# Cross-attention's queries called a unit ahead, and value differences made from rows copied one row down by DMA

## The chip, the cores and the metric

The kernel runs on one core of one Trainium2 chip. The metric is device time in microseconds (us) of one execution, and the time before is the median of three runs.

The core has five engines with their own instruction queues: PE (matrix multiplications and transposes), DVE (vector), ACT (scalar), POOL and SP. In this kernel SP only issues DMA transfers, mostly loads; POOL computes a little and issues nearly all stores. Each engine takes its instructions strictly in the order of its queue: an instruction that waits holds all behind it. The transfers themselves are moved by 16 DMA engines that SP's and POOL's queues share.

## What is computed

One layer of a hybrid encoder, for a prompt of 2048 rows and a sample of 64 rows, all in float32:

```python
h = rms_norm(x, g_norm)
z = h @ w_in                      # 24 chunks of 128 columns: q, k, v, gate of branch A; u, gate of B; q, gate of C
o_sb   = stick_breaking(q_sb, k, v)             # branch A, 8 heads of 64
o_pool = multiscale_pool(u) @ pool_w * scale    # branch B
o_xa   = softmax(q_xa @ mk.T / 8) @ mv          # branch C: cross-attention to 256 memory rows, 4 heads of 64
y = rms_norm(x + concat[o_sb*silu(g_sb), o_pool*silu(g_pool), o_xa*silu(g_xa)] @ w_out, g_final)
```

The new keys and values (rows by head) are outputs too. In branch A the kernel does not use the values themselves but the differences between neighbouring rows, `v[t-1] - v[t]` (with a row of zeros ahead of the first), so that the running products of the stick-breaking weights need no further multiplication.

## The kernel before, in words

**Split products.** Float32 products are made of three passes of PE with the operands split into a high and a low part (lines 427 to 429). One "piece" is such a product for one of the 8 slices of the contraction; a "block" is 8 pieces (24 multiplications): one chunk of 128 columns of z for 512 rows of the prompt. Four blocks (n = 0 to 3) make a chunk; the last is wider, as the sample's 64 rows go with it.

**The stage that is changed** makes 4 chunks of keys and then 4 chunks of values: 32 blocks, 16 of keys and 16 of values. After a block of keys or values, ACT copies the accumulator to SBUF (`zf`, `zv`), POOL stores it transposed as it is (`vt_d`), PE turns it into rows (`pt_r`, line 463), ACT copies these rows to the tile `rt` (line 465), and POOL stores them to the output. The tile `rt` has **one buffer**, so ACT's next copy to it waits until all readers of the last one are done. The accumulator and most others have two.

**Value differences before.** POOL subtracts neighbouring columns of the transposed values (`dz`, line 564; the first column comes from the block before by a small copy on DVE, line 556), PE turns the result into rows with four more transposes (`pt_d`, line 570), ACT copies them (line 571), and POOL stores them to `dv_d` (line 572).

**Cross-attention** is interleaved with these blocks in 16 units of 256 query rows and two heads: scores (line 764, 765), softmax (DVE, ACT), transposes (`pt_p`), products with the memory values (`avx`), a gate on POOL and a store. The queries were stored earlier to `qx_d` and are loaded by SP (line 748). Each load of 256 KB reads 64 rows twice, through a leading dimension of size 2 and step 0, so that both halves of the 128 partitions get the same queries. Two such loads (one for each head) and one of the gate (`sg_x`, line 751) make a unit's loads.

**What sets the order.** A small helper, `Slots`, counts pieces: `slots.after(d, f)` runs `f` d pieces later. A unit starts with every second block (16 pieces), its stages follow after the delays in XSLOTS, and the next unit's loads are called 12 pieces after a unit's start. Behind this, the framework's scheduler orders each engine's queue, moves instructions by its own estimates, and adds the semaphore waits. After the values a new set of buffers is opened for the sample's work, which waits for the stage's last users.

Of the kernel before, what the change touches and what calls it, by code (L numbers as in the profile page):

```python
# [8 lines left out]
F32 = mybir.dt.float32  # L9
F32R = mybir.dt.float32r  # L10
# [3 lines left out]
ALU = mybir.AluOpType  # L14
# [4 lines left out]
P = 128  # L19
# [9 lines left out]
NB = T // 512  # L29
UNIT = 256  # L30
# [7 lines left out]
def f(ap):  # L38

    return ap.bitcast(F32)  # L40
# [3 lines left out]
def tile_hybrid_step(  # L44
# [30 lines left out]
    V, A, G, PE = nc.vector, nc.scalar, nc.gpsimd, nc.tensor  # L75
    dma, store = nc.sync.dma_start, nc.gpsimd.dma_start
# [7 lines left out]
    v_new = sb_v_prompt[0, 0].rearrange("t h d -> t (h d)")  # L84
# [11 lines left out]
    ident = edge[:, 384:]  # L96
# [9 lines left out]
    vt_d = [dram.tile([P, T], F32, name=f"vt_d{p}") for p in range(4)]  # L106
    sg_d = [dram.tile([P, T], F32, name=f"sg_d{p}") for p in range(6)]
# [56 lines left out]
    def join(av, out, odd):  # L164

        own, other = (HI, LO) if odd else (LO, HI)
        A.copy(out[own], av[other])
        V.tensor_tensor(out[own], av[own], out[own], ALU.add)
# [81 lines left out]
    class Stream:  # L250
# [35 lines left out]
        def piece(self):  # L286

            if not self.pieces:
                self.pieces += self.more()
            if self.pieces:  # L290
                thunk = self.pieces.pop(0)
                if thunk is not None:
                    thunk()
                    return True
            return False
# [40 lines left out]

    slots, ROWS, XSLOTS = Slots(), 2, (1, 7, 13, 16, 17, 20)


    hpool = ctx.enter_context(tc.tile_pool(name="hpool", bufs=1))
# [2 lines left out]
    ps_t = ctx.enter_context(tc.tile_pool(name="ps_t", bufs=2, space=PSUM))  # L345
# [17 lines left out]
    st = st0 = scope.enter_context(tc.tile_pool(name="st0", bufs=2))  # L363
# [34 lines left out]
    def load_ahead():  # L398

        if order:  # L400
            c = order.pop(0)
            loaded[c] = split_weights(win[:, c * P : (c + 1) * P].rearrange("(k p) m -> p k m", p=P), wpool)

    def chunk_of(c):
        while c not in loaded:
            load_ahead()
        return loaded.pop(c)
# [42 lines left out]
    def project(w, n, chunk):  # L450
        for piece in projection(w, n, chunk):
            acc = piece()
            slots.tick()
        return acc

    def halves(t):
        return t.rearrange("p (a b) -> p a b", a=2)

    def rows_of(src, out, n_tiles):

        pt = ps_t.tile([P, 4, P], F32, tag="pt", name="pt_r")
        for j in range(n_tiles):
            PE.transpose(pt[:, j], src[:, j * P : (j + 1) * P], ident)
        rt = st.tile([P, n_tiles, P], F32, tag="rt", name="rt", bufs=1)
        A.copy(rt[:, :n_tiles], pt[:, :n_tiles])
        store(out.rearrange("(j p) c -> p j c", p=P), rt[:, :n_tiles])
        return rt
# [56 lines left out]
    def tokens(n):  # L524
        return slice(512 * n, 512 * n + 512)
# [24 lines left out]
        slots.after(ROWS, lambda: rows_of(zf, k_new[tokens(n), p * P : (p + 1) * P], 4))  # L550

    def values(acc, n, p):

        zv = st.tile([P, 1 + 512], F32, tag="zf", name="zv")
        if n:
            V.tensor_copy(zv[:, 0:1], last_values[0][:, 512:])
        else:
            V.memset(zv[:, 0:1], 0.0)
        last_values[:] = [zv]
        A.copy(halves(zv[:, 1:]), acc)  # L560
        store(vt_d[p][:, tokens(n)], zv[:, 1:])
        two = st.tile([P, 2, 512], F32, tag="s", name="dv")
        dz, dr = two[:, 0], two[:, 1].rearrange("p (j c) -> p j c", j=4)
        G.tensor_tensor(dz, zv[:, :512], zv[:, 1:], ALU.subtract)

        def rows():
            rows_of(zv[:, 1:], v_new[tokens(n), p * P : (p + 1) * P], 4)
            pt = ps_t.tile([P, 4, P], F32, tag="pt", name="pt_d")
            for j in range(4):
                PE.transpose(pt[:, j], dz[:, j * P : (j + 1) * P], ident)  # L570
            A.copy(dr, pt)
            store(dv_d[p][:, n], dr)

        slots.after(ROWS, rows)

    last_values = []

    mxs = normed([mem_prompt[0, :P, :]], P, gm, "m0", lambda: dma(gm, g_mem[0:1, :].broadcast_to([P, D])))
    mxs += normed([mem_prompt[0, P:, :]], P, gm, "m1")
# [16 lines left out]
    for n in range(NB):  # L596
        turns = norm_group(n + 1) if n + 1 < NB else []
        for p in range(2):
            pieces = projection(w2[p], n, QX0 + p)
            for k, piece in enumerate(pieces):  # L600
                acc = piece()
# [10 lines left out]
    st = scope.enter_context(tc.tile_pool(name="st1", bufs=2))  # L612
# [22 lines left out]
    for c in range(2):  # L635
        for j in range(2):
            w, rows = WINDOWS[2 * c + j], slice(64 * j, 64 * j + 64)
# [65 lines left out]
    for c in range(2):  # L703
        w = chunk_of(U0 + c)
        last, pls = None, []
        for n in range(NB):
            acc = project(w, n, U0 + c)
            u = st.tile([P, HIST + 512], F32, tag="u", name="u")
# [12 lines left out]
        for n in (3, 0, 1, 2):  # L721
            acc = project(w, n, GP0 + c)
            sg = st.tile([P, 512], F32, tag="zf", name="sg_p")
# [14 lines left out]
    st = scope.enter_context(tc.tile_pool(name="st2", bufs=2))  # L738
    xa = mscope.enter_context(tc.tile_pool(name="xa", bufs=1))

    def cross_loads(p, u):

        cols = slice(UNIT * u, UNIT * u + UNIT)
        qx = []
        for j in range(2):
            q = xa.tile([P, 2, UNIT], F32R, tag=f"q{j}", name="qx", bufs=2)
            src = qx_d[p][HI if j else LO, :, cols]
            dma(f(q), src.unsqueeze(0).broadcast_to([2] + list(src.shape)))
            qx.append(q)
        sg = xa.tile([P, UNIT], F32, tag="sg", name="sg_x", bufs=2)  # L750
        dma(sg, sg_d[4 + p][:, cols])
        return qx, sg

    def cross(p, u, loads):

        qx, sg = loads
        pr, turned = [None] * 2, [None] * 2
        o = xa.tile([P, UNIT], F32, tag="ox", name="ox")

        def scores(i):  # L760
            q = slice(P * i, P * i + P)
            s = ps_x.tile([P, 2, NMEM], F32, tag="x", name="sx")
            for j in range(2):
                PE.matmul(s[:, j], qx[j][:, 0, q], mks[2 * p + j], start=True, stop=False)
                PE.matmul(s[:, j], qx[j][:, 1, q], mks[2 * p + j], start=False, stop=True)
            pr[i] = xa.tile([P, 2, NMEM], F32, tag=f"pr{i}", name="pr")
            softmax(s, P, pr[i])

        def turn(j):
            pt = ps_t.tile([P, 2, 2, P], F32, tag="pt", name="pt_p")  # L770
            for b in range(2):
                for i in range(2):
                    PE.transpose(pt[:, b, i], pr[i][:, j, b * P : (b + 1) * P], ident)
            ph = xa.tile([P, 2, UNIT], F32R, tag="ph", name="ph")
            pl = xa.tile([P, 2, UNIT], F32R, tag="plo", name="plo")
            ptf = pt.rearrange("p b i q -> p b (i q)")
            A.copy(ph, ptf)
            V.tensor_tensor(pl, ptf, f(ph), ALU.subtract)
            turned[j] = ph, pl

        def gather(j):
            av = ps_x.tile([P, 512], F32, tag="y", name="avx")
            ph, pl = turned[j]
            for b in range(2):
                mv = mvs[p][:, b, 2 * j : 2 * j + 2].rearrange("p a d -> p (a d)")
                PE.matmul(av[:, :UNIT], mv, ph[:, b], start=(b == 0), stop=False)
                PE.matmul(av[:, :UNIT], mv, pl[:, b], start=False, stop=(b == 1))
            join(av[:, :UNIT], o, j)
            if j:
                G.tensor_tensor(o, o, sg, ALU.mult)  # L790
                store(mix_d[u // 2][:, 6 + p, UNIT * (u % 2) : UNIT * (u % 2) + UNIT], o)

        for delay, stage, i in zip(XSLOTS, (scores, scores, turn, gather, turn, gather), (0, 1, 0, 0, 1, 1)):
            slots.after(delay, lambda stage=stage, i=i: stage(i))

    crosses = [(p, u) for p in range(2) for u in range(T // UNIT)]
    loads = cross_loads(*crosses[0])

    def next_cross():
        def ahead():  # L800
            nonlocal loads
            if crosses:
                loads = cross_loads(*crosses[0])

        cross(*crosses.pop(0), loads)
        slots.after(12, ahead)

    for make, c0 in ((keys, K0), (values, V0)):
        for p in range(4):
            w = chunk_of(c0 + p)  # L810
            for n in range(NB):
                if n % 2 == 0:
                    next_cross()
                make(project(w, n, c0 + p), n, p)
                if n == 0:
                    load_ahead()
# [5 lines left out]
    st = scope.enter_context(tc.tile_pool(name="st3", bufs=2))  # L822
# [131 lines left out]
    st = ctx.enter_context(tc.tile_pool(name="st4", bufs=2))  # L954
# [6 lines left out]
    for c0, m0, m in ((G0, 0, 4), (GX0, 6, 2)):  # L961
        sg = st.tile([P, 4, TS], F32, tag="sgs", name="sg_s", bufs=1)
# [52 lines left out]
    loads = []  # L1015
# [183 lines left out]
```

## Time and profile before

| what | value |
|---|---|
| median of 3 runs | 1418.0 us (1412.6 to 1421.86) |
| time of the profiled execution | 1418.25 us |
| span of its instructions | 1416.5 us |
| mean granted TensorE clock | 0.971 of full speed |
| stage of keys and values in the span | about 255 to 545 us |

The profile is of one execution. Its page gives each engine's busy time, the chain of work that ended last, and the costliest groups of instructions. Further views of the same trace answer for a stretch of time: the busy time and granted clock in given windows, who waited for whom, the instructions in order of time, the DMA queues with the packets and bytes that they moved, and the chain of waits. "<-" after an idle time names what ended it.

### The profile page before, as it was taken

The page shows a single profiled execution, that of the slowest core. Times are in us where ns is not written, and L with a number is a line of the kernel's source. Part 1 is how long each engine was busy: PE and PEld are TensorE (multiplying, and loading weights), DVE is VectorE, ACT ScalarE, POOL GpSimd, SP SyncE. Part 2 cuts the span into 40 slices and gives each one's busy share as a digit, 9 for nine tenths or more (in the row PEclk, how much of TensorE's full clock was granted, in tenths as well). Part 3 has the DMA queues.
Part 4 walks back from the last instruction along what each step waited for, and adds up shares of the span by engine and source line. Part 5 has one row for each costly group of instructions (what it writes and reads, how often), then busy time and mean ns, then how long its engine had stood idle before and what let it go on. Part 6 is the DMA issues. An engine that isn't in the chain of part 4 may idle for free.

```text
span 1416.5 us, 19689 instructions
## 1 busy us (share of the span) xinstructions
PE 1305.2 (92%) x7418; PEld 986.6 (70%) x7418; DVE 757.9 (54%) x1315; ACT 553.4 (39%) x1141; POOL 322.6 (23%) x425
## 2 busy tenths in 40 slices
PE   5999999699999999999999989999999989999976
PEld 5788877488888888788876656655665656666554
DVE  7853446154444443243234666657676677787523
ACT  5631110143334442221123545455454555655521
POOL 2111336143444442231001232211110011010031
PEclk9999999799999999999999999999999999999988
DMA  7635253244444444433257853334343343331031
GB/s 230 199 114 161 95 185 110 98 155 152 165 156 155 153 140 138 140 107 127 77 193 242 290 178 130 112 108 139 93 129 102 114 144 96 103 107 56 2 116 70
DMA packets 114682, 190.66 MB, mean 135 GB/s; under 512 B 8450, under 2 KB 73052, under 8 KB 114588
## 3 DMA queue, kind: packets, MB, share of 16 engines
q1 hardware_dynamic: 93772, 119.11, 27.5%
q0 software_dynamic: 20816, 70.30, 13.5%
q8 instruction: 58, 0.95, 0.3%
q14 instruction: 36, 0.29, 0.1%
HBM read 119.10 MB, written 70.29 MB: 134 GB/s over the span
## 4 chain that ended last, share of the span: by engine, by line
PE 50%; issue 19%; DMA 12%; DVE 9%; POOL 6%; ACT 2%; SPq 1%; POOLq 0%; DVEq 0%; ACTq 0%
PE acc L1073 7%; PE acc L427 7%; PE acc L428 7%; PE acc L429 7%; PE av L235 6%; DMA qx<-qx_d 6%; PE pt L221 6%; PE z L198 5%; DVE at_hl L210 2%; PE z L1073 2%; DMA m<-mix_d 2%; POOL psum_w L655 2%; DMA mix_d<-ends 1%; PE pt_x L389 1%; DVE wl L420 1%
## 5 line engine op out<-in xcount | busy, mean ns | idle before, releaser
L427 PE MATMUL acc<-hh,wh 128*128 128x512 f32 (+2 forms) x960 | 360.5, 376 | 6.4 <-DVE sg L529 5.6
L428 PE MATMUL acc<-hl,wh 128*128 128x512 f32 (+2 forms) x960 | 344.0, 358 | 0.0
L429 PE MATMUL acc<-hh,wl 128*128 128x512 f32 (+2 forms) x960 | 342.9, 358 | 0.0
L210 DVE TENSOR_TENSOR_SCAN at_hl<-at_hl,at_hl 128x512 f32<-128x512 f32 x148 | 182.2, 1282 | 58.0 <-ACT at_hl L203 57.9
L427 PEld LDWEIGHTS acc<-hh,wh 128*128 128x128 f32 x960 | 183.3, 191 | 33.5 <-DVE sg L529 7.8
L429 PEld LDWEIGHTS acc<-hh,wl 128*128 128x128 f32 x960 | 182.8, 191 | 24.5 <-issue 0.7
L428 PEld LDWEIGHTS acc<-hl,wh 128*128 128x128 f32 x960 | 183.6, 191 | 20.8 <-issue 3.8
L221 PE MATMUL pt<-edge,at_hl 128*128 128x128 f32 x968 | 150.7, 279 | 13.2 <-ACT at_hl L223 9.3
L221 PEld LDWEIGHTS pt<-edge,at_hl 128*128 128x128 f32 x968 | 114.8, 141 | 58.3 <-ACT at_hl L223 17.8
L235 PE MATMUL av<-more_w,at_hh 128*64 128x512 f32 (+2 forms) x480 | 139.0, 538 | 4.6 <-ACT more_w L223 4.6
L203 ACT ACTIVATE at_hl<-z 128x1024 f32<-128x1024 f32 (+3 forms) x143 | 122.4, 890 | 47.5 <-PE z L198 46.7
L223 ACT COPY more_w<-pt 128x512 f32<-128x512 f32 (+2 forms) x240 | 118.4, 517 | 34.5 <-PE pt L221 32.9
L208 DVE TENSOR_TENSOR_SCAN at_hl<-at_hl,edge 128x128 f32<-128x128 f32 (+3 forms) x116 | 86.7, 805 | 53.8 <-ACT at_hl L203 53.7
L1073 PE MATMUL acc<-at_hh,mh 128*128 128x512 f32 x208 | 95.1, 457 | 10.4 <-DVE xo L1076 10.4
L223 ACT COPY at_hl<-pt 128x512 f32<-128x512 f32 x80 | 43.4, 542 | 129.7 <-PE pt L221 129.7
L1059 POOL TENSOR_TENSOR ml<-m,mh 128x256 fp32r<-128x256 f32 x64 | 53.1, 853 | 148.7 <-ACT mh L1058 148.4
L247 POOL TENSOR_TENSOR ends<-ends 128x512 f32<-128x512 f32 x16 | 21.3, 1332 | 283.3 <-DVE ends L246 193.3
L1073 PE MATMUL acc<-at_hl,mh 128*128 128x512 f32 (+1 forms) x208 | 84.6, 411 | 0.0
L198 PE MATMUL z<-at_hh 64*128 64x512 f32 (+2 forms) x576 | 82.3, 398 | 0.2 <-ACT at_hl L203 0.2
L235 PE MATMUL av<-at_hl,at_hh 128*64 128x512 f32 (+1 forms) x160 | 79.9, 581 | 0.6 <-DVE ends L246 0.6
L1073 PE MATMUL acc<-at_hh,ml 128*128 128x512 f32 x192 | 77.3, 402 | 0.0
L235 PEld LDWEIGHTS av<-more_w,at_hh 128*64 128x64 f32 x480 | 39.9, 139 | 45.9 <-issue 22.0
(257 smaller groups left out, 1887.5 us busy)
## 6 DMA issues: line engine op xcount, KB each, us to landing
at_hh<-k_d SPq DMA_DIRECT2D x40, 512.0 KB
wr<-in_w_in_dram SPq DMA_DIRECT2D x24, 512.0 KB
at_hh<-dv_d SPq DMA_DIRECT2D x40, 256.0 KB
xt_x<-in_x_prompt_dram SPq DMA_DIRECT2D x16, 512.0 KB
qx<-qx_d SPq DMA_DIRECT2D x32, 256.0 KB
k_d<-k POOLq DMA_DIRECT2D x16, 512.0 KB, 6.1
out_dram<-rt POOLq DMA_DIRECT2D x32, 256.0 KB, 5.7
q_d<-q POOLq DMA_DIRECT2D x16, 512.0 KB, 3.0
```

The lines of the kernel that those rows point to most:

```text
L198: PE.matmul(z[:, h, :w], a["q"][rows, part, at], K[rows, keys, :w], start=(part == keys == 0), stop=(part == 1),)
L203: A.activation(c[:, :, :n], z[:, :, :n], AF.Sigmoid, scale=-1.0)
L208: V.tensor_tensor_scan(cc, cc, edge[:, 512 - n :][:, ::-1], 0.0, ALU.mult, ALU.max)
L210: V.tensor_tensor_scan(cc, cc, cc, self.later[i][:, h, 0:1], ALU.mult, ALU.bypass)
L221: PE.transpose(pt[:, i], self.cs[i][:, h, kb * P : kb * P + P], ident)
L223: A.copy(w[:, i0:], pt[:, i0:])
L235: PE.matmul(a["av"][rows, i0 * P :], self.V[:, kb, rows], turned[h][:, i0:], start=(self.diag and kb == 0), stop=(j == 0 and kb == 3),)
L427: PE.matmul(out, wh[:, k], hi, start=(k == 0), stop=False)
L428: PE.matmul(out, wh[:, k], lo, start=False, stop=False)
L429: PE.matmul(out, wl[:, k], hi, start=False, stop=(k == KT - 1))
L1059: G.tensor_tensor(ml, m, f(mh), ALU.subtract)
L1073: PE.matmul(o, m, w, start=(c == i == 0), stop=(c == 7 and i == len(passes) - 1))
```

## The change

Two things are changed in the stage of keys and values.

**Cross-attention.** The loaded queries and gates no longer come from pools but from two fixed buffers each, taken in turn. A unit starts every 15 pieces instead of every 16, the first after 8 pieces; when a unit is started the queries of the following one are called at once. The gate is called by the unit itself, 6 pieces after its start. Most stages of a unit stand one piece nearer to its start than before.

**Value differences.** The four transposes, ACT's copy, DVE's copy of the first column and the subtraction of columns are removed. Instead SP copies the rows tile `rt` one row down, from SBUF to SBUF, into a tile `dr`: rows 0 to 126 to rows 1 to 127 (line 566), the last row of tiles 0 to 2 to the first row of tiles 1 to 3 (line 567), and the last row of tile 3 to the first row of the next block's `dr` (line 569, not for the last block of a chunk). POOL then subtracts `rt` from `dr` (line 570) and stores the result. `rt` still has one buffer.

```diff
--- before.py
+++ after.py
@@ -336,7 +336,7 @@
 
 
 
-    slots, ROWS, XSLOTS = Slots(), 2, (1, 7, 13, 16, 17, 20)
+    slots, ROWS, XSLOTS = Slots(), 2, (1, 6, 12, 15, 16, 19)
 
 
     hpool = ctx.enter_context(tc.tile_pool(name="hpool", bufs=1))
@@ -550,30 +550,29 @@
         slots.after(ROWS, lambda: rows_of(zf, k_new[tokens(n), p * P : (p + 1) * P], 4))
 
     def values(acc, n, p):
-
-        zv = st.tile([P, 1 + 512], F32, tag="zf", name="zv")
-        if n:
-            V.tensor_copy(zv[:, 0:1], last_values[0][:, 512:])
-        else:
-            V.memset(zv[:, 0:1], 0.0)
-        last_values[:] = [zv]
-        A.copy(halves(zv[:, 1:]), acc)
-        store(vt_d[p][:, tokens(n)], zv[:, 1:])
-        two = st.tile([P, 2, 512], F32, tag="s", name="dv")
-        dz, dr = two[:, 0], two[:, 1].rearrange("p (j c) -> p j c", j=4)
-        G.tensor_tensor(dz, zv[:, :512], zv[:, 1:], ALU.subtract)
-
-        def rows():
-            rows_of(zv[:, 1:], v_new[tokens(n), p * P : (p + 1) * P], 4)
-            pt = ps_t.tile([P, 4, P], F32, tag="pt", name="pt_d")
-            for j in range(4):
-                PE.transpose(pt[:, j], dz[:, j * P : (j + 1) * P], ident)
-            A.copy(dr, pt)
+        zv = st.tile([P, 512], F32, tag="zf", name="zv")
+        A.copy(halves(zv), acc)
+        store(vt_d[p][:, tokens(n)], zv)
+
+        if n == 0:
+            above[:] = [st.tile([P, 8, P], F32, tag="s", name="dv")[:, :4]]
+            V.memset(above[0][0:1, 0], 0.0)
+        dr = above.pop()
+        if n < NB - 1:
+            above.append(st.tile([P, 8, P], F32, tag="s", name="dv")[:, :4])
+
+        def rows(nxt=list(above)):
+            rt = rows_of(zv, v_new[tokens(n), p * P : (p + 1) * P], 4)
+            dma(dr[1:], rt[: P - 1])
+            dma(dr[0:1, 1:], rt[P - 1 :, :3])
+            for t in nxt:
+                dma(t[0:1, 0], rt[P - 1 :, 3])
+            G.tensor_tensor(dr, dr, rt, ALU.subtract)
             store(dv_d[p][:, n], dr)
 
         slots.after(ROWS, rows)
 
-    last_values = []
+    above = []
 
     mxs = normed([mem_prompt[0, :P, :]], P, gm, "m0", lambda: dma(gm, g_mem[0:1, :].broadcast_to([P, D])))
     mxs += normed([mem_prompt[0, P:, :]], P, gm, "m1")
@@ -743,17 +742,16 @@
         cols = slice(UNIT * u, UNIT * u + UNIT)
         qx = []
         for j in range(2):
-            q = xa.tile([P, 2, UNIT], F32R, tag=f"q{j}", name="qx", bufs=2)
+            q = xroom(f"q{j}")
             src = qx_d[p][HI if j else LO, :, cols]
             dma(f(q), src.unsqueeze(0).broadcast_to([2] + list(src.shape)))
             qx.append(q)
-        sg = xa.tile([P, UNIT], F32, tag="sg", name="sg_x", bufs=2)
-        dma(sg, sg_d[4 + p][:, cols])
-        return qx, sg
-
-    def cross(p, u, loads):
-
-        qx, sg = loads
+        return qx
+
+    def cross(p, u, qx):
+
+        sg = xroom("sg")
+        slots.after(6, lambda: dma(sg, sg_d[4 + p][:, UNIT * u : UNIT * u + UNIT]))
         pr, turned = [None] * 2, [None] * 2
         o = xa.tile([P, UNIT], F32, tag="ox", name="ox")
 
@@ -793,24 +791,30 @@
         for delay, stage, i in zip(XSLOTS, (scores, scores, turn, gather, turn, gather), (0, 1, 0, 0, 1, 1)):
             slots.after(delay, lambda stage=stage, i=i: stage(i))
 
+    xrings = {
+        name: [xa.tile([P, 2, UNIT] if name != "sg" else [P, UNIT], F32R if name != "sg" else F32, name=f"x{name}{i}") for i in range(2)]
+        for name in ("q0", "q1", "sg")
+    }
+
+    def xroom(name):
+        xrings[name].append(xrings[name].pop(0))
+        return xrings[name][-1]
+
     crosses = [(p, u) for p in range(2) for u in range(T // UNIT)]
-    loads = cross_loads(*crosses[0])
+    called = [cross_loads(*crosses[0])]
 
     def next_cross():
-        def ahead():
-            nonlocal loads
-            if crosses:
-                loads = cross_loads(*crosses[0])
-
-        cross(*crosses.pop(0), loads)
-        slots.after(12, ahead)
-
+        cross(*crosses.pop(0), called.pop(0))
+        if crosses:
+            called.append(cross_loads(*crosses[0]))
+
+
+    for i in range(len(crosses)):
+        slots.after(8 + 15 * i, next_cross)
     for make, c0 in ((keys, K0), (values, V0)):
         for p in range(4):
             w = chunk_of(c0 + p)
             for n in range(NB):
-                if n % 2 == 0:
-                    next_cross()
                 make(project(w, n, c0 + p), n, p)
                 if n == 0:
                     load_ahead()
```

How instructions stand in the queues is shown at three places. First the queue of **SP** in the stretch of the values (`qx`, `xq` are queries, `sg_x`, `xsg` gates, `wr` weights). Before:

```order
L748 DMA qx<-qx_d_78 128x2x256 x2
L411 DMA wr<-in_w_in_dram 128x8x128
L751 DMA sg_x<-sg_d_92 128x256
L748 DMA qx<-qx_d_78 128x2x256 x2
L751 DMA sg_x<-sg_d_92 128x256
```

With the change, for a like stretch (`rt` are the rows, `dv` the tile with the shifted rows):

```order
L747 DMA xq_2341<-qx_d_78 128x2x256
L747 DMA xq_2343<-qx_d_78 128x2x256
L754 DMA xsg_2344<-sg_d_92 128x256
L566 DMA dv<-rt 127x512
L567 DMA dv<-rt 1x16x24
L569 DMA dv<-rt 1x16x8
L411 DMA wr<-in_w_in_dram 128x8x128
L566 DMA dv<-rt 127x512
```

16 copies of 127 rows, 16 and 12 copies of parts of one row now stand between the loads of queries, gates and weights. From the first copy of 127 rows to the last there are five pairs of query loads.

Second the queue of **POOL** for the first block of values. Before:

```order
L561 DMA vt_d_83<-zv 128x512
L564 TENSOR_TENSOR dv<-zv 128x512
L466 DMA out_dram<-rt 128x4x128
L572 DMA dv_d_79<-dv 128x512
L561 DMA vt_d_83<-zv 128x512
```

With the change:

```order
L555 DMA vt_d_83<-zv 128x512
L466 DMA out_dram<-rt 128x4x128
L570 TENSOR_TENSOR dv<-dv,rt 128x512
L571 DMA dv_d_79<-dv 128x512
L555 DMA vt_d_83<-zv 128x512
```

The subtraction now reads the rows and the shifted rows, so it stands behind SP's copies; the next block's store of `zv` stands behind it.

Third the queue of **PE** at the first scores of cross-attention. Before:

```order
L463 MATMUL pt_r<-edge,zf 128x128 x4
L427 MATMUL acc<-hh_128,wh 128x512
L428 MATMUL acc<-hl_132,wh 128x512
L764 MATMUL sx<-mks_137,qx 128x256
L765 MATMUL sx<-mks_137,qx 128x256
L429 MATMUL acc<-hh_128,wl 128x512
```

With the change:

```order
L463 MATMUL pt_r<-edge,zf 128x128 x4
L427 MATMUL acc<-hh_128,wh 128x512
L428 MATMUL acc<-hl_132,wh 128x512
L762 MATMUL sx<-mks_137,xq_2340 128x256
L763 MATMUL sx<-mks_137,xq_2340 128x256
L429 MATMUL acc<-hh_128,wl 128x512
```

The first scores stand at the same place as before; those of the second unit stand 12 multiplications of `acc` later than before, after the rows of the second block.

## Rows read from the trace of the kernel before

**Rows 1.** The page's first lines: span, and busy time and share of engines.
```profile
span 1416.5 us, 19689 instructions
PE 1305.2 (92%) x7418; PEld 986.6 (70%) x7418; DVE 757.9 (54%) x1315; ACT 553.4 (39%) x1141; POOL 322.6 (23%) x425
```

**Rows 2.** Busy time in three stretches (start, keys, values), clock, DMA share, GB/s.
```profile
262.00:292.00 30.00, 16.53 (x68) 12.41 (x69) 6.57 (x17) 7.15 (x18) 4.42 (x5) 0.72 0.26 91
292.00:411.00 119.00, 112.41 (x675) 99.30 (x674) 56.48 (x131) 44.84 (x122) 49.96 (x59) 0.99 0.46 158
411.00:541.00 130.00, 122.57 (x758) 106.29 (x756) 54.62 (x128) 54.50 (x140) 53.02 (x75) 1.00 0.44 148
```

**Rows 3.** Waits of PE, keys stretch: us in total, times, longest us.
```profile
PE sx L764 <- DMA qx<-qx_d: 19.7, 6, 8.5
```

**Rows 4.** PE in order of time: start, us, instruction [idle before it].
```profile
271.55 0.55 PE L764 MATMUL sx<-mks,qx 128*128 128x256 f32 x1 [8.50 <-DMA qx<-qx_d]
...
277.03 0.58 PE L764 MATMUL sx<-mks,qx 128*128 128x256 f32 x1 [3.86 <-DMA qx<-qx_d]
```

**Rows 5.** Waits of PE, values stretch.
```profile
PE pt_d L570 <- POOL dv L564: 5.0, 9, 0.6
PE pt_d L570 <- DVE sm_m L153: 2.6, 3, 0.9
```

**Rows 6.** Groups of PE in the values stretch: count | busy, mean ns.
```profile
L570 PE MATMUL pt_d<-edge,dv 128*128 128x128 f32 x60 | 9.7, 283 | 7.4 <-POOL dv L564 4.8 <-DVE sm_m L153 2.6
```

**Rows 7.** Line 465 in the values stretch: ns min/median/max, first and last start.
```profile
L465 ACT COPY rt<-pt_r x16: 585/585/592, 412.2 to 541.4; 128x512 f32<-128x512 f32 x16
```

**Rows 8.** DMA queues, 277 to 281 us: packets, MB, share of 16 engines.
```profile
DMA packets 184, 0.19 MB, mean 47 GB/s; under 512 B 0, under 2 KB 184, under 8 KB 184
...
q1 hardware_dynamic: 184, 0.19, 13.5%
```

**Rows 9.** DMA queues, 398 to 399 us.
```profile
q0 software_dynamic: 93, 0.31, 80.9%
q1 hardware_dynamic: 46, 0.05, 13.4%
```

**Rows 10.** POOL in order of time, one block of values.
```profile
424.46 0.73 POOL L790 TENSOR_TENSOR ox<-ox,sg_x 128x256 f32<-128x256 f32 x1 [0.46 <-DVE ox L168]
...
428.29 1.05 POOL L564 TENSOR_TENSOR dv<-zv 128x512 f32<-128x512 f32 x1
429.75 0.78 POOL L466 DMA_DIRECT2D out_dram<-rt  x1 [0.41 <-ACT rt L465]
```

**Rows 11.** Chain of waits, end of the stage: start, us, what.
```profile
545.73 2.71 DMA mix_d<-ox
...
548.90 2.25 DMA cmk<-in_cache_mem_k_dram
551.15 0.24 issue
```

**Rows 12.** DMA issues: count, KB each, us to landing.
```profile
qx<-qx_d SPq DMA_DIRECT2D x32, 256.0 KB
...
out_dram<-rt POOLq DMA_DIRECT2D x32, 256.0 KB, 5.7
...
vt_d<-zv POOLq DMA_DIRECT2D x16, 256.0 KB, 5.3
dv_d<-dv POOLq DMA_DIRECT2D x16, 256.0 KB, 5.4
...
cmk<-in_cache_mem_k_dram SPq DMA_DIRECT2D x2, 128.0 KB
```

## The prediction

> **What bounds the kernel now.** I read the page first: PE is busy for 92% of the span [rows 1], so the question in any stretch is what keeps PE waiting there. The stage of keys and values is cut in three [rows 2]. In its first 30 us (262 to 292) PE is busy for 16.5 us and its granted clock is 0.72, which is a mix of 2.4 and 1.2 GHz; in the keys (292 to 411) it is busy for 112.4 of 119 us, in the values (411 to 541) for 122.6 of 130, at a clock of 0.99 and 1.00. So PE sets the pace of both long stretches, and only the first is bound by something else. The waits say what: in the keys PE waited 19.7 us for query loads, six times [rows 3], and 12.4 us of this are the first two scores, 8.50 and 3.86 us [rows 4]. The other four waits are 7.3 us together. In the values PE waits for no load, only before the transposes of differences, 5.0 and 2.6 us [rows 5].
>
> The pace of the values is read from ACT's copies of rows: 16 of them start between 412.2 and 541.4 us [rows 7], 15 intervals of **8.61 us**.
>
> The third thing to see is how fast a transfer moves. From 277 to 281 us only query loads run. They move 47 GB/s and fill 13.5% of 16 engines [rows 8], which is 2.2 engines, at 47 / 2 = 23.5 GB/s each. Their leading dimension has size 2. A microsecond of stores elsewhere fills 80.9% of 16 engines, about 13, with 0.31 MB [rows 9], 24 GB/s each. So an engine's rate is the same in both, and the query loads are slow because they use two engines.
>
> **The queries called ahead.** This can remove the 7.3 us of later waits, since a load gets a whole unit more. It does not remove the first 12.4 us: the first scores stand in PE's queue where they stood, and the first two loads are still SP's first in the stage. Nor can it remove more by its amount, since the same 32 loads [rows 12] are made. A pair moves 512 KB, at 47 GB/s 11.2 us, and a unit of 15 pieces lasts 15/16 of two blocks, some 16 us at the values' pace. That is enough. I take **-7 us**; the ends are 0 (the pairs, sharing the queue with weights and gates, stay late) and -13 (the first stretch, idle for 13.5 of its 30 us [rows 2], shrinks by some 6 as well).
>
> **What the values lose.** The differences' transposes are 9.7 us for 15 blocks [rows 6], and the waits before them 7.6 us [rows 5]: 0.65 and 0.51 us a block. Without them a block would take PE 8.61 - 1.16 = 7.45 us. ACT's copy and DVE's small copy go as well; both engines have slack (54.5 and 54.6 of 130 us busy [rows 2]), so I cost them at nothing.
>
> **What the values get.** The tile of rows has one buffer. ACT's next copy to it must wait until POOL's subtraction has read it, and this until SP's copies have landed. So there is a loop once a block, and if it takes longer than 7.45 us it sets the pace. Its terms:
>
> - ACT's copy of rows: 0.6 us [rows 7].
> - A load's fixed part. The chain has 2.25 us for a load of 128 KB over 128 rows [rows 11, 12]; 16 engines at 23.5 GB/s move that in 0.35 us, so 1.9 us is left.
> - Moving 127 rows of 2 KB, 260 KB. The trace has no copy of 127 rows and none from SBUF to SBUF, so this is bounded: 0.7 us if it is spread over 16 engines, 260 KB / 23.5 GB/s = 11.1 us if it stays on one. The nearest row is the query load, a transfer of SP's queue whose engines were as many as its leading dimension let them be shared evenly: 2 of 2 [rows 8]. 127 is prime, so an even share means one engine. I take **11.1 us**.
> - The two copies of parts of a row behind it, in the same queue: between 0 and another 1.9 us of fixed part; they are small and are issued while the large one moves, so 0.5.
> - POOL's subtraction: 1.05 us, the same size as the one removed [rows 10].
> - Three handovers between engines at 0.24 to 0.46 us each [rows 10, 11]: 0.9.
> - POOL's three stores of 256 KB in a block [rows 12] put 16 KB each on every engine, 0.7 us at 23.5 GB/s, so 0 to 2.1 us where they meet the copy; 1.0.
>
> Sum: 0.6 + 1.9 + 11.1 + 0.5 + 1.05 + 0.9 + 1.0 = **17.0 us** a block. Fifteen intervals cost 15 x (17.0 - 8.61) = **+126 us**.
>
> The rule behind the third term is in the Trainium skill, "DMA: Bandwidth & Descriptors", section "Why a DMA increments its semaphore by 16 and not by 1": SP's transfers run on the largest number of engines up to 16 that divides the slowest dimension of both sides, and 127 partitions are named there as a case of one engine, the lowest-numbered. The trace agrees for the size 2, with 13.5% of 16 engines; no run here shows 127. By the rule the sum is as above; if the row of size 2 were only a matter of the repeated source, the third term would be 0.7.
>
> **What is queued behind.** SP's queue is in order. That the two engines of the query loads include the copy's is not shown by a row; I assume it, and the lower end below stands for the other case. Five pairs of loads stand between copies. A pair takes 11.2 us of moving (13 with a start for each), and the loop leaves the engine free for 17.0 - 11.1 - 1.0 = 4.9 us a block. So a pair puts the next copy off by 6.3 to 8.1 us: five times, **+35 us** (10 if they use the rest of the time better, 65 if nothing overlaps). On POOL the next store of `zv` stands behind the subtraction; it frees a buffer of two, and its block has the same 17 us, so nothing is added. On ACT everything behind the waiting copy of rows is late, and PE stops when accumulators and transposes have no free buffer. PE's work of 7.45 us a block would be 14.9 us at the clock's lower level of 1.2 GHz, still under 17.0: the cover is thin, and if waits add to it PE takes part in the bound.
>
> **The end of the stage.** Before, the last rows are copied at 541.4 us and the next stage's first load is issued at 548.9 [rows 7, 11]. With the loop the last block still has the copy, subtraction and store after its rows, about 17 + 3 us instead of 7.5, less a few us of query projections that PE has meanwhile: **+10 us** (0 to 12).
>
> Sum: -7 + 126 + 35 + 10 = +164. The profiled execution took 1418.25 us, a quarter of a us above the median, with 1.75 us outside its span; nothing outside changes. 1418 + 164 = **1582 us**.
>
> **Rivals.**
>
> A, the other side: **the copy is spread over 16 engines**. Then the loop is 17.0 - 11.1 + 0.7 = 6.6 us, under PE's 7.45, and the change gives what it removes: 16 x 1.16 = 18.6 and 7 us of query waits, 1418 - 26 = 1392. It decides where the copy moves in less than 7.45 - 5.9 = 1.5 us, which is 8 engines or more. For it: all copies of 128 rows run on many engines [rows 9]. Against it: the query loads have 128 rows at their destination too and run on two [rows 8]. Chance 0.13.
>
> B, **nothing overlaps**: the small copies have a fixed part of their own (+1.4), all three stores fall on the copy's engine in its time (+1.1), so 19.5 us a block, and the query pairs add 13 us each. 15 x 10.9 + 65 + 10 - 7 = +231, 1649. For it: the waits of an in-order queue add up. Against it: stores and loads come from two queues that ran side by side in [rows 9]. Chance 0.12.
>
> C, **one engine moves twice as fast from SBUF to SBUF** as from memory: 5.6 us, a loop of 11.5 us, 15 x 2.9 = 43, with 35, 5 and -7: 1494. Two rates near 24 GB/s, for loads and for stores [rows 8, 9], speak against it; no row has both sides in SBUF. Chance 0.05.
>
> **How the numbers follow.** My forecast has a chance of 0.70. Its lowest sum has a loop of 15.3 us (no small copies, no meeting stores, handovers of 0.2 us), 10 for the query pairs, no end and -13: about +97, or 1515. Its highest is B's loop with larger handovers, 1665. The range goes down to 1500 for a part of C and up to 1665; A and the rest of C lie outside. About 1% is what a measurement of this kernel can tell from no change: A lies under that, so faster has 0.12, and 0.03 is left for the same, where A's gain is half eaten by POOL waiting on the copies' landing. Slower has 0.85.
>
> **What would show it.** Right: in the values the rows' copies on ACT start some 17 us apart, longer where query loads stand between; ACT's wait before line 465 is the longest and is put down to POOL's subtraction, and this waits for DMA; stretches in which only line 566's copy moves show about 6% of 16 engines, packets of 2 KB; the granted clock falls in the values; the first scores still wait about 12 us. Wrong: copies that land 3 us after their issue, and blocks of 7.5 us in the values. Then rival A holds, and the step that failed is the number of engines.

## The result, and the profile after

The changed kernel takes **1637.15 us** (median of 4 runs, 1632.74 to 1639.43) against 1418.08 us before (median of 4): a ratio of 1.154 (95% interval 1.151 to 1.156). The forecast was 1582 us in a range of 1500 to 1665, so the direction, the mechanism of the loop and the range held, and the size was 55 us short. The profiled execution took 1632.74 us; the account below is of that one, with a span 214.5 us longer than before (1631.0 against 1416.5).

The page's first lines, against [rows 1]: PE's share of the span falls from 92% to 82%, with almost the same busy time.

```profile
span 1631.0 us, 19630 instructions
PE 1331.4 (82%) x7354; PEld 1009.4 (62%) x7354; DVE 756.2 (46%) x1303; ACT 543.5 (33%) x1125; POOL 323.4 (20%) x425
```

The stage by stretches (us, busy time and count of PE, PEld, DVE, ACT and POOL, granted clock, DMA share, GB/s), against [rows 2]. The stretches are the keys, the wait for the first shifted rows, and the values:

```profile
300.00:418.00 118.00, 107.58 (x614) 93.62 (x614) 58.56 (x126) 43.07 (x115) 44.16 (x54) 0.96 0.45 150
418.00:448.00 30.00, 14.84 (x86) 12.65 (x84) 3.27 (x9) 3.64 (x9) 1.72 (x3) 0.79 0.20 65
448.00:748.00 300.00, 146.00 (x684) 126.13 (x684) 45.73 (x109) 42.07 (x113) 54.60 (x73) 0.71 0.22 71
```

In the values PE works for 146 of 300 us, at a granted clock of 0.71, a mix of its two levels, and the DMA engines are busy for only 22%. Neither is the bound; something in series is. ACT's waits in the values name it: before its copies of rows (line 465, as in [rows 7]) it waited 206.8 us for POOL's subtraction, which had itself waited for the copies.

```profile
ACT rt L465 <- POOL dv L570: 206.8, 14, 22.3
```

```profile
POOL dv L570 <- DMA dv<-rt: 252.3, 15, 27.4
POOL dv L570 <- DMA xq<-qx_d: 21.5, 1, 21.5
```

One round of this loop stands in the chain of waits (start, us, what), from one subtraction to the next, 692.26 to 709.90 us:

```profile
692.26 1.27 POOL dv L570
693.52 0.02 issue
693.55 0.59 ACT rt L465
694.14 0.02 issue
694.16 0.64 SPq L566
694.80 0.04 issue
694.85 14.88 DMA dv<-rt
...
709.90 1.26 POOL dv L570
```

And a stretch in which nothing but the copy of 127 rows moves (the DMA queues from 441 to 446 us, packets, MB, share of 16 engines), against [rows 8]:

```profile
DMA packets 60, 0.12 MB, mean 25 GB/s; under 512 B 0, under 2 KB 0, under 8 KB 60
...
q1 hardware_dynamic: 60, 0.12, 6.5%
```

6.5% of 16 is one engine; 60 packets of 2 KB in 5 us are 83 ns each, 10.6 us for 127.

### The profile page after: what moved, and what is told of

The parts are those of the page before. It is cut to its first block, busy times and chain, and to the rows that moved or that the text cites. A ratio compares the mean times of both kernels' runs of the same rounds, so it can differ in the third digit from the quotient of the medians.

```text
span 1631.0 us, 19630 instructions
## 1 busy us (share of the span) xinstructions
PE 1331.4 (82%) x7354; PEld 1009.4 (62%) x7354; DVE 756.2 (46%) x1303; ACT 543.5 (33%) x1125; POOL 323.4 (20%) x425
## 4 chain that ended last, share of the span: by engine, by line
PE 32%; DMA 27%; issue 12%; DVE 6%; POOL 3%; SPq 2%; ACT 2%; POOLq 0%; DVEq 0%; ACTq 0%
DMA dv<-rt 15%; DMA xq<-qx_d 8%; PE acc L1077 6%; PE av L235 5%; PE pt L221 5%; PE z L198 4%; PE acc L427 3%; PE acc L428 3%; PE acc L429 3%; DVE at_hl L210 3%; PE z L1077 2%; POOL dv L570 1%; DMA m<-mix_d 1%; SPq L754 1%; DMA mix_d<-ends 1%
## 5 line engine op out<-in xcount | busy, mean ns | idle before, releaser
L427 PE MATMUL acc<-hh,wh 128*128 128x512 f32 (+2 forms) x960 | 369.6, 385 | 5.7 <-DVE sg L529 4.7
L428 PE MATMUL acc<-hl,wh 128*128 128x512 f32 (+2 forms) x960 | 352.1, 367 | 0.0
L429 PE MATMUL acc<-hh,wl 128*128 128x512 f32 (+2 forms) x960 | 349.2, 364 | 0.0
L427 PEld LDWEIGHTS acc<-hh,wh 128*128 128x128 f32 x960 | 190.6, 199 | 34.7 <-DVE sg L529 6.8
L429 PEld LDWEIGHTS acc<-hh,wl 128*128 128x128 f32 x960 | 189.2, 197 | 25.8 <-issue 0.7
L428 PEld LDWEIGHTS acc<-hl,wh 128*128 128x128 f32 x960 | 190.7, 199 | 22.0 <-issue 3.8
L465 ACT COPY rt<-pt_r 128x512 f32<-128x512 f32 (+1 forms) x36 | 20.2, 561 | 228.1 <-POOL dv L570 206.8
L771 PE MATMUL pt_p<-edge,pr 128*128 128x128 f32 x128 | 24.2, 313 | 74.7 <-DVE pr L162 65.9
```

The lines of the kernel that those rows point to most:

```text
L427: PE.matmul(out, wh[:, k], hi, start=(k == 0), stop=False)
L428: PE.matmul(out, wh[:, k], lo, start=False, stop=False)
L429: PE.matmul(out, wl[:, k], hi, start=False, stop=(k == KT - 1))
```

## The experiments

**The cut at 112 rows.** 112 rows have 16 even shares of 7, the 15 others one each.

```diff
-            dma(dr[1:], rt[: P - 1])
+            dma(dr[1:113], rt[:112])
+            dma(dr[113:], rt[112 : P - 1])
```

> The copy of 127 rows is cut into one of 112 and one of 15 rows; all else is the changed kernel, and SP's queue has the same order with one transfer more a block. Theory E (the copy's time is set by how many engines share its rows evenly: 127 is prime, so one; 112 has 16 shares, 15 has 15): the 12 us of moving fall under 1 us, the loop falls from 18 us to 7 or 8, and the values are back at PE's pace. The query pairs still hold two of the 16 engines for 11 us, which can put a copy off: 1395 to 1440 us, 1415 the likeliest. Rival F (copies from SBUF to SBUF, or their place in SP's queue, are slow however they are shared): the loop keeps 17 us or more, as there is one transfer more: 1620 to 1650 us.

Measured: 1480.34 us, a ratio to before of 1.045 (1.042 to 1.048), 157 us less than the changed kernel. Rival F falls. In the window of the first copy (432.4 to 434.2 us) SP's queue fills 61% of 16 engines instead of 6.5%:

```profile
q1 hardware_dynamic: 248, 0.33, 61.0%
```

The time lies above the expected range of 1395 to 1440, though. POOL's subtractions (start, us, idle time before) come in rounds of two sorts:

```profile
438.66 1.26 POOL L571 TENSOR_TENSOR dv<-dv,rt 128x512 f32<-128x512 f32 x1 [18.69 <-DMA dv<-rt]
446.19 1.27 POOL L571 TENSOR_TENSOR dv<-dv,rt 128x512 f32<-128x512 f32 x1 [2.51 <-DMA dv<-rt]
462.95 1.25 POOL L571 TENSOR_TENSOR dv<-dv,rt 128x512 f32<-128x512 f32 x1 [13.35 <-DMA dv<-rt]
...
592.35 1.29 POOL L571 TENSOR_TENSOR dv<-dv,rt 128x512 f32<-128x512 f32 x1 [3.92 <-DMA dv<-rt]
599.77 1.29 POOL L571 TENSOR_TENSOR dv<-dv,rt 128x512 f32<-128x512 f32 x1 [2.34 <-DMA dv<-rt]
607.06 1.28 POOL L571 TENSOR_TENSOR dv<-dv,rt 128x512 f32<-128x512 f32 x1 [3.86 <-DMA dv<-rt]
```

At the end, where no query load is left, a round takes 7.3 to 7.4 us, which is the forecast's 7.45 us of PE. From 446.19 to 462.95 it takes 16.8, as a pair of queries and a gate stand between in SP's queue (start, us of issue):

```profile
443.89 2.43 SPq L748 DMA_DIRECT2D xq<-qx_d  x2
446.37 8.88 SPq L755 DMA_DIRECT2D xsg<-sg_d  x1
455.37 0.58 SPq L566 DMA_DIRECT2D dv<-rt  x1
```

The gate's issue is held 8.9 us behind the queries, and the copy cannot be issued before 455.37.

**The cut at 113 rows**, a control: the same two transfers in the same places.

```diff
-            dma(dr[1:], rt[: P - 1])
+            dma(dr[1:114], rt[:113])
+            dma(dr[114:], rt[113 : P - 1])
```

> The same cut one row later: 113 and 14 rows, the same number of transfers in the same order, the same bytes. 113 is prime, 14 has 14 even shares. Theory E: the 113 rows stay on one engine, 113 x 2 KB in about 9.5 to 12 us, so the loop loses only a ninth of its moving: 1610 to 1640 us. Rival F has no reason for a difference to the cut at 112: the same time as that run within 1%.

Measured: 1621.93 us in a single run. One row more, 142 us more than the cut at 112. The copy of 113 rows is on one engine again; the same 5 us as above (438 to 443 us), with the small pieces among its packets:

```profile
DMA packets 106, 0.12 MB, mean 25 GB/s; under 512 B 46, under 2 KB 46, under 8 KB 106
...
q1 hardware_dynamic: 106, 0.12, 7.0%
```

So it is neither the size, the SBUF on both sides, nor the number of transfers: on SP's queue the number of rows must have an even share.

**The copy issued by POOL.**

```diff
-            dma(dr[1:], rt[: P - 1])
+            store(dr[1:], rt[: P - 1])
```

> The changed kernel with its copy of 127 rows issued by POOL and not by SP; the two copies of parts of a row stay on SP. If the number of rows alone decides (127 has no even share), the copy stays on one engine and the loop stays about 18 us, though query loads no longer stand ahead of it in its queue: 1560 to 1640 us. If it is the way SP's queue shares rows, the copy falls to 1 or 2 us of moving, and it is no more held behind query loads: 1420 to 1480 us.

Measured: 1475.64 us in a single run: the second case. POOL's copies of the same 127 rows land 3.4 to 7.3 us after their issue, 4.5 in the median, and the quiet rounds take 7.5 to 7.6 us (583.82 to 591.41 is one):

```profile
583.82 1.28 POOL L570 TENSOR_TENSOR dv<-dv,rt 128x512 f32<-128x512 f32 x1 [3.08 <-DMA dv<-rt]
...
587.43 0.54 POOL L566 DMA_DIRECT2D dv<-rt  x1
591.41 1.29 POOL L570 TENSOR_TENSOR dv<-dv,rt 128x512 f32<-128x512 f32 x1 [3.43 <-DMA dv<-rt]
```

The rule of one engine is thus one of SP's queue. The Trainium skill, "DMA: Bandwidth & Descriptors", section "Why a DMA increments its semaphore by 16 and not by 1", has this too, as an exception for some direct copies issued from POOL, which put 127 partitions on engines 0 to 15; this run agrees as far as landings go, which are under the 10.6 us that one engine needs, and shows no count of engines. The time was no better than with the cut, as the queries' delay was not removed by another queue for this copy alone: the copies of parts of a row were still behind them on SP, and each round still waits for those. In one such round POOL's copy is issued at 449.33 us, but the parts only at 456.09, behind a gate whose issue took 9.64 us, and the subtraction starts at 462.79.

**Two buffers for the rows tile**, the copy of 127 rows as it was.

```diff
-        rt = st.tile([P, n_tiles, P], F32, tag="rt", name="rt", bufs=1)
+        rt = st.tile([P, n_tiles, P], F32, tag="rt", name="rt", bufs=2)
```

> The rows tile gets two buffers; the copy of 127 rows stays as it is. Theory E with the loop through the single buffer: ACT's copy no longer waits for the subtraction, so the copies follow each other and the one engine's own work sets the pace: 10.6 us of copy, 1 to 2 of stores, 3.5 of queries a block, about 16 instead of 21 us: 1545 to 1575 us. If the single buffer does not matter, because POOL's and SP's queues are in order anyway, nothing changes: 1625 to 1645 us.

Measured: 1598.35 us in a single run, 39 us less, half of what was expected and in neither range. The subtractions show why:

```profile
444.98 1.26 POOL L570 TENSOR_TENSOR dv<-dv,rt 128x512 f32<-128x512 f32 x1 [28.78 <-DMA dv<-rt]
457.74 1.28 POOL L570 TENSOR_TENSOR dv<-dv,rt 128x512 f32<-128x512 f32 x1 [7.73 <-DMA dv<-rt]
482.26 1.26 POOL L570 TENSOR_TENSOR dv<-dv,rt 128x512 f32<-128x512 f32 x1 [21.10 <-DMA dv<-rt]
...
682.44 1.26 POOL L570 TENSOR_TENSOR dv<-dv,rt 128x512 f32<-128x512 f32 x1 [8.69 <-DMA dv<-rt]
695.14 1.27 POOL L570 TENSOR_TENSOR dv<-dv,rt 128x512 f32<-128x512 f32 x1 [8.42 <-DMA dv<-rt]
```

The quiet rounds fell from 18 to between 12.3 and 14.4 us, so the loop did run through the single buffer. What is left is the copy's own time on its engine: near the end the 508 packets of four copies follow each other without a gap, in 51.1 us, 12.8 for each with the stores among them. The rounds with queries kept their 24 to 30 us: there the copy stands behind the queries in SP's queue, and no buffer helps.

**The query part alone** (values as before).

```diff
-        zv = st.tile([P, 512], F32, tag="zf", name="zv")
+        zv = st.tile([P, 1 + 512], F32, tag="zf", name="zv")
...
+        two = st.tile([P, 2, 512], F32, tag="s", name="dv")
+        dz, dr = two[:, 0], two[:, 1].rearrange("p (j c) -> p j c", j=4)
+        G.tensor_tensor(dz, zv[:, :512], zv[:, 1:], ALU.subtract)
...
```

> The cross-attention part of the change alone; the value differences are made as before. In the changed kernel the first rows of values were copied at 418.45 us, 6.3 us later than before, and PE's waits for queries were 23.5 us against 19.7. If this comes from the queries' order (they hold the queue and two engines whenever they are called), the kernel is 2 to 10 us slower than before: 1420 to 1428 us. If it came from the values' copies ahead in SP's queue, the queries alone give what I forecast, 1405 to 1415 us.

Measured: 1416.57 us, a ratio of 1.0006 (0.9986 to 1.0026): no difference. Both expectations miss, one by a little on either side. Calling the queries ahead gained nothing: PE's waits for them in the keys stayed what they were, 19.8 against 19.7 us [rows 3], and the first rows of values are copied 0.9 us earlier than before [rows 7].

```profile
PE sx L763 <- DMA xq<-qx_d: 19.8, 7, 8.5
...
411.25 0.59 ACT L465 COPY rt<-pt_r 128x512 f32<-128x512 f32 x1 [0.80 <-PE pt_r L463]
```

**The value part alone** (cross-attention as before; the rest is the change's own diff).

> The value part of the change alone, with cross-attention as before. Theory E: nearly the whole loss is here, as the query part alone was the same as before within 0.3%: 1620 to 1650 us. If the queries' new order makes the values' loss worse (the gates and queries between the copies), it is 1580 to 1615 us.

Measured: 1630.57 us in a single run: the first case. The loss is the value part's. A part of it lies ahead of the values: the first rows of values are copied 6.2 us later than before [rows 7], though the queries are called as before.

```profile
418.39 0.59 ACT L465 COPY rt<-pt_r 128x512 f32<-128x512 f32 x1 [0.30 <-ACT pr L156]
```

**Query loads of 64 rows**, first in the changed kernel, whose copy of 127 rows stays. Both halves are loaded by a transfer of their own; nothing else moves.

```diff
-            dma(f(q), src.unsqueeze(0).broadcast_to([2] + list(src.shape)))
+            for half in (LO, HI):
+                dma(f(q[half]), src)
```

> The changed kernel with its copy of 127 rows on one engine, but the query loads made of two loads of 64 rows. Theory E: every block of values takes the quiet loop of 17.6 to 18.9 us instead of 22 in the mean (15 x 4 = 60 us less), the first copy is not held 12 us behind queries, and 20 us of waits in the keys go: 1637 - 85 = 1552, 1540 to 1570 us. If the loop's longer rounds came from elsewhere (stores, weights), 1600 to 1640 us.

Measured: 1561.88 us in a single run, 75 us less: the first case. The first subtraction starts at 404.33 us instead of 447.52, the last at 686.23 instead of 764.67. So between the two profiled executions, 71 us apart, 43 us had been lost before the first shifted rows were there and 35 after; behind the last subtraction 8 us go the other way. The first case had about 32 before and 60 after, so that its total came out is partly luck.

The same two lines in the kernel before:

> The kernel before with only the query loads made of two loads of 64 rows. Theory E: the first scores wait 2 or 3 us for a load instead of 8.5, the other five waits go, and the first stretch keeps the higher clock: 1390 to 1402 us. If the loads were late because they are called late and not because they are slow, 1412 to 1420 us.

Measured: **1388.54 us**, a ratio of 0.980 (0.978 to 0.982), a little under the first case. PE's waits for queries in the keys fall from 19.7 us to

```profile
PE sx L765 <- DMA qx<-qx_d: 1.5, 1, 1.5
```

and the granted clock from 262 to 292 us is 1.00 instead of the 0.72 of [rows 2]. The loads were late because they were slow, not because they were called late.

**Both mended:** the cut at 112 and the query loads of 64 rows.

> The cut at 112 rows, and each query load made of two loads of 64 rows (one for each half of the partitions) instead of one with a leading dimension of 2. In the run with the cut alone the blocks without query loads between took 7.3 to 8.1 us, those with them about 15, as the next copy was issued 9 us late behind them. Theory E (what is left is the query loads' two engines): they move in 1 us instead of 11, the values run at PE's pace of 7.45 us (16 x 1.16 = 18.6 us less than before), and most of PE's 20 us of waits for queries go: 1375 to 1400 us, 1383 the likeliest. Rival Q (what is left is SP's queue, in order and now with still more transfers in it): 1450 to 1485 us.

Measured: 1393.44 us, 0.983 (0.981 to 0.985). Rival Q falls. It is within the range, but 5 us above the run with the queries alone on the same chip, 1390.18 to 1395.78 against 1387.82 to 1389.44. The loop is still there, at the edge: ACT waited 25.5 us for the subtraction.

```profile
ACT rt L465 <- POOL dv L571: 25.5, 10, 4.2
```

**With two buffers for the rows as well**, with the queries called as in the change and as before:

> The run with the cut at 112 rows and query loads in two halves, and two buffers for the rows tile. Without them ACT waited 25.5 us for POOL's subtraction before its copies of rows, and the kernel took 1393 us where the one before with only the query loads mended took 1389. Theory E with the loop through the single buffer: this wait goes and most of it comes off the time: 1372 to 1388 us. If in-order POOL (waiting for the copies' landing, stores behind it) sets the pace, nothing moves: 1388 to 1398 us.

> The same, but with cross-attention's units called as in the kernel before (every 16 pieces, loads called 12 pieces into the unit). If calling the queries ahead is worth nothing once they move on 16 engines, the same time as its sister run within 0.5%; if it is worth something, 5 to 15 us slower than that.

Measured: 1386.26 us, 0.980 (0.977 to 0.983), and **1382.04 us**, 0.977 (0.974 to 0.981). The wait of ACT is gone in the first, and the time moved from its sister without the buffer by 7 us between two chips, with intervals that overlap, so what the second buffer is worth here is not shown. Calling the queries ahead is worth nothing; the old order is 0.3% better. The last version is faster than both kernels. Whether its shifted copies are worth anything over the transposes is open: 0.977 and 0.980 (the queries alone) were measured on different chips, with intervals that overlap.

## Why the prediction was right, and where its size was off

**The number of engines**, the step on which all hung, was right: one. The cut at 112 against 113 shows it alone, 1480 against 1622 us. Rival A's mechanism, the spread copy, was built twice (the cut, and POOL's queue) and does what A said for the quiet rounds, 7.3 to 7.6 us, PE's 7.45. It did not give A's 1392 us, but 1480 and 1476: A's sum lacked some 85 us of copies that stand behind queries in SP's queue. With the queries mended as well it is 1393 us, which is no better than the queries mended alone.

**The loop** was forecast at 17.0 us. The eight quiet rounds of the profile are 17.6 to 18.9 us, 18.0 in the mean. The parts in the chain above: 14.9 us from the copy's issue done to its landing, with 0.64 of issue, where the forecast had 1.9 + 11.1 + 0.5 + 1.0 = 14.5 in all; the subtraction takes 1.26 us and not the 1.05 of [rows 10], now that it reads two tiles and writes over one of them; the handovers are smaller than the 0.9 taken. 15 x 1.0 = 15.5 us short. Rival B's 19.5 us did not come: the stores do lengthen a copy, but by 0.7 to 3.2 us of 10.6 (the packets of the copies issued from 676.45 to 729.94 us take 11.2 to 13.8 us), and the small copies cost nearly nothing.

**The queries between copies**: five rounds held a pair, as counted. They took 23.8 to 30.2 us, 38 us over quiet rounds; forecast 35.

**A wait that the prediction had not**: four weight loads (line 411) also stand between copies. Two of them had to wait, and their rounds took 4.9 and 4.0 us more than a quiet one. The chain of waits shows the first (start, us, what):

```profile
490.27 1.27 POOL dv L570
491.54 0.29 issue
491.82 2.78 DMA dv_d<-dv
...
494.74 0.15 DVE dv L559
494.89 0.59 DVE wh L418
...
497.21 0.14 SPq L411
...
497.45 0.66 SPq L566
```

The next chunk's tile of shifted rows is set to zero by DVE (line 559), which waits until the tile's last content is stored; DVE's splitting of weights stands behind it, SP's weight load waits for that, and the next copy stands behind this load. In the second, ACT's copy of rows was held behind DVE's queue too, until 675.79 us, so the two cannot be told apart there. The forecast said what is queued behind on SP, but took the queue's loads as issued when their turn came.

**The queries called ahead** was the step that failed: "-7 us", on the ground that a pair's 11.2 us are less than a unit's 16. The query part alone gained 0.9 us up to the first rows of values and nothing in time, so the term was mis-sized by 6 to 7 us. In the changed kernel PE still waited 23.5 us for queries up to there, the first two scores 9.08 and 4.02 against [rows 4]. SP's issues of pairs (start, us) show why:

```profile
331.05 9.87 SPq L747 DMA_DIRECT2D xq<-qx_d  x2
...
347.83 11.45 SPq L747 DMA_DIRECT2D xq<-qx_d  x2
...
367.07 8.92 SPq L747 DMA_DIRECT2D xq<-qx_d  x2
...
387.12 6.23 SPq L747 DMA_DIRECT2D xq<-qx_d  x2
...
400.45 8.19 SPq L747 DMA_DIRECT2D xq<-qx_d  x2
```

From 331.05 to the next pair, at 415.72 (below), there are five intervals of 17 us in the mean, in which SP's queue is never free for more than 1.8 us: with a gate and weights between, a pair takes the queue longer than a unit of 15 pieces takes PE. The 16 us of the forecast were the values' pace; in the keys, where these units run, a block takes 7.5 us once the loads are fast (the kernel before with query loads of 64 rows copies rows at 296.32 and, ten blocks on, at 371.60), so 15 pieces are 14 us. A load that is the bound cannot be hidden by calling it earlier.

**The keys became longer with the value part**, which the forecast did not have. The first rows of values were copied at 418.45 us, 6.3 us later than before [rows 7] and 7.2 later than with the query part alone. The value part alone has the same delay, 418.39, with the queries called as before. It is gone where the query loads are fast: with loads of 64 rows and the old calls, those rows are copied at 386.81 us without the value part and at 386.12 with it (the last version, cut at 112 rows and with two buffers). How a part that starts behind the keys slows their loads is not shown.

**The first copy** had no term either. It was ready to be issued after the rows of 418.45 us and was issued at 431.41, behind a pair and a gate:

```profile
415.72 9.73 SPq L747 DMA_DIRECT2D xq<-qx_d  x2
425.50 5.69 SPq L754 DMA_DIRECT2D xsg<-sg_d  x1
431.41 0.69 SPq L566 DMA_DIRECT2D dv<-rt  x1
```

Its subtraction came 29.1 us after the rows instead of 16.7, 12.4 us more.

**The end** was forecast at +10: from the last rows to the next stage's first load it took 21.1 us (748.21 to 769.31) instead of 7.5, so +13.6; what follows was 5.9 us shorter.

Together, what the profile has over the forecast: 15.5 for the loop, 3 for queries between, 9 for weights, 12.4 for the first copy, 6.1 for the queries called ahead and 7.2 for the longer keys, 3.6 - 5.9 at the end: 51 us, of 50.7 between the profiled 1632.7 and 1582. Why what follows the stage was 5.9 us shorter is not shown. The first copy, the queries between copies and the two terms of the keys, 29 us, have the slow query loads in common: the forecast priced a load by what it moves on its engines, and not by how long it holds SP's queue with all that stands behind it. Query loads of 64 rows take 75 us off, which shows what the slow loads cost in all; time spent moving and time spent holding the queue go together there, so that run does not tell the two apart.

## What to carry to other kernels

Before a transfer is put on SP's queue, look at the outermost size on both sides: 127 rows went to one engine and a leading dimension of 2 to two, and cutting them into 112 + 15 (in the changed kernel) or 64 + 64 (in the one before) took 157 and 30 us off. A tile that is copied, waited for and overwritten in one buffer makes a loop whose whole latency is paid once a block, however idle the engines. And a slow transfer is paid twice: for itself and for whatever stands behind it in an in-order queue, so price a queue by how long each issue is held.

## What the runs showed of the hardware

The transfer behind a one-engine copy is not only late to land, its issue is held: in the values SP's issue right behind the copy of 127 rows took 5.5 to 8.0 us in 14 of 16 blocks, against 0.5 to 1.2 for the same issue in the cut version.

```profile
694.85 6.32 SPq L567 DMA_DIRECT2D dv<-rt  x1
```

The subtraction on POOL of 128x512 elements took 1.05 to 1.06 us when both operands were shifted views of one tile and the result went to another, and 1.25 to 1.29 us in the median of each run with two tiles, one of them written over (single ones up to 1.90). Which of the two differences makes it longer is not shown.
